# Block 2's attention in units of one query tile between projection steps, split value sums, and filter taps on ScalarE with adding DMAs

## The chip, the cores and the metric

The kernel runs on one core of a Trainium2 chip. The metric is the device time of one execution in microseconds (us). A core has five engines with a queue each: TensorE (PE) for matrix products, with its weight loads (PEld) shown apart; VectorE (DVE); ScalarE (ACT); GpSimd (POOL); and SyncE (SP), which here only starts transfers. Sixteen DMA engines move the data.

## What is computed

Two transformer blocks on 512 tokens of width 1024, in float32. Block 1 has an mLSTM and a sliding-window attention, a cross attention and a convolved feed-forward. Block 2 has four mixers of width 256 each that read the same projection, an output projection and a feed-forward. The change lies in block 2's mixers:

```
u_conf, u_sc, u_att, u_lru = split(rms_norm(x, pre_mix_g) @ w_in)
# conf: z = val * sigmoid(gate); causal depthwise filter of 31 taps; group norm; silu
y_a = conformer_conv_mixer(u_conf, ...)
# short conv: b_gate * causal_depthwise_conv(c_gate * xs, 3 taps)
y_b = short_conv_mixer(u_sc, ...)
# attention: 4 heads of width 64, blocks of 256 keys, slopes on the distance, causal
y_c = moba_attention(u_att)
# gated linear recurrence after a causal filter of 4 taps
y_d = rglru_mixer(u_lru, ...)
y = concatenate([y_a, y_b, y_c, y_d]) @ w_out
x = x + rms_norm(y, post_mix_g)
```

With 512 tokens there are two key blocks, and all earlier keys are attended to: the attention is a plain causal one of 512 by 512 with a bias by distance.

## The kernel before

**Split products.** A float32 product of full precision is made of three fp32r passes: each operand is split into a high part (`split`, line 112, on ACT) and the remainder (line 113, on DVE), and PE adds high x high, high x low and low x high (`mm3`, lines 138 to 140; `tm_phase`, lines 223 to 227). Weights come by SP's DMAs of 1 MB into three raw buffers and are split into five pairs of weight tiles (`split_w`).

**Block 2's mixers.** `X3` holds the normalised input, channels on partitions, split. `cm_phase` (from line 153) makes one column chunk of 128 outputs after the other: split its weights, 24 matmuls of 512 columns into one PSUM bank, then an evacuation function. The chunks are, in order: the filter's gates and values and the first recurrence gate (five, the first ones in halves), then the attention's queries and keys (`ATT`, four), the attention's values (`tm_block`), and nine in `rest`. The attention's score product is likewise split: the query tile `aq(h)` has the high half on 64 partitions and the low half on the other 64, and `ak(h)` gives two key tiles, so that two matmuls make a tile's scores. They live in the slots 0, 1, 4 and 5 of `H3`, the split concatenated mixer output, and in `akp`.

**The attention.** `at_head(h)` (line 1175) makes for four query tiles: two score matmuls, a reduction with bias and minimum on DVE (line 1185), the exponential with its sum on ACT (line 1187), reciprocal and normalisation on DVE (lines 1188 and 1189), transposes on PE with float32 operands (line 1192) and a copy out of PSUM, on DVE and ACT in turn (line 1193). Then four matmul groups in float32 (line 1243) add up a head's values; the trace shows each as two instructions. After each head some of the nine `rest` chunks are made (`cuts`), and the recurrence (`lru`), the group norm's mean (`conf_mean`) or its end (`conf_norm`).

**The filter.** `taps(c)` (line 1118) puts 31 DVE instructions for each of the two channel chunks into the list `bg`: each multiplies a shifted input `zp` by a weight and adds it to `acc`. `pump(n)` (line 149) writes the next n of them into the program; `cm_phase` calls it after each chunk, and the rest is written before `conf_mean`.

**What sets the order.** The program is written as a list of instructions for each engine and goes through a planner (`TileContext(schedule_with_timeline_sim=True)`, line 1401). It places the instructions by simulated time: the one written first goes first, but one written later may go ahead while the first is not ready in the plan. On the chip the order of an engine's queue is then fixed: an instruction that waits holds those behind it. Buffers of a tag (`bufs`) come round; whoever takes one waits until its last user is done.

**What follows.** `w_out` (line 1287, `tm_phase`) reads `H3` in the order of `order4`, slots 6, 7, 2, 3, 4, 5, 0, 1: recurrence, short convolution, attention, filter. Its first group is of two token tiles, with 12 matmuls for each slot. Of its eight weight tiles the last three are in the extra pool `wx4`.

Of the kernel before, what the change touches and what calls it, by code (L numbers as in the profile page):

```python
# [41 lines left out]
def tile_two_blocks(ctx: ExitStack, tc: tile.TileContext, a: dict, out: bass.AP, dbg=None):  # L42
# [988 lines left out]
    def tmp():  # L1031
        return mx.tile([P, T], F32, name="tmp", tag="tmp", bufs=6)
# [41 lines left out]
    cs, cx = {}, {}  # L1074

    def sc_c(c):
        def f(ps):
            cs[c], cx[c] = tmp(), tmp()
            act.activation(cs[c], ps, AF.Copy)
        return f  # L1080

    def sc_x(c):
        def f(ps):
            dve.tensor_mul(cx[c], cs[c], ps)
            w = pv[:, c, SCW:SCW + 3]
            act.activation(cs[c], cx[c], AF.Copy, scale=w[:, 2:3])
            for j in (1, 0):
                s = 2 - j
                dve.scalar_tensor_tensor(cs[c][:, s:], cx[c][:, :T - s], w[:, j:j + 1], cs[c][:, s:],
                                         op0=OP.mult, op1=OP.add)  # L1090
        return f

    def sc_b(c):
        def f(ps):
            dve.tensor_mul(cx[c], cs[c], ps)
            split(H3[0][:, 2 + c, :], H3[1][:, 2 + c, :], cx[c])
        return f
# [20 lines left out]
    def taps(c):  # L1118
        z, w = zp[c], half[:, c, :]
        bg.append(lambda: dve.tensor_scalar(acc[c], z[:, 0:T], w[:, 0:1], pv[:, c, DWB:DWB + 1],  # L1120
                                            op0=OP.mult, op1=OP.add))
        for j in range(1, 31):
            bg.append(lambda j=j: dve.scalar_tensor_tensor(acc[c], z[:, j:j + T], w[:, j:j + 1], acc[c],  # L1123
                                                           op0=OP.mult, op1=OP.add))
# [3 lines left out]
    def conf_mean():  # L1128
        for c in (1, 0):
# [22 lines left out]
    def lru(c):  # L1152
# [13 lines left out]
        dve.tensor_mul(lps[0], av_, av_)  # L1166
# [8 lines left out]
    def at_head(h):  # L1175
        pts = m2.tile([P, NT, T], F32, name="apts", tag="apts", bufs=1)
        for i in range(NT):
            n = (i + 1) * P
            s = psm.tile([P, T], F32, name="as", tag="s", bufs=2)
            m = max(n, 256)  # L1180
            for j in range(2):
                pe.matmul(s[:, :m], aq(h)[:, i * P:(i + 1) * P], ak(h)[j][:, :m], start=j == 0, stop=j == 1)
            L = m2.tile([P, T], F32, name="aL", tag="aL", bufs=2)
            st = m2.tile([P, 3], F32, name="ast", tag="ast", bufs=4)
            dve.tensor_tensor_reduce(L[:, :n], s[:, :n], ab[:, T - n:], scale=-0.25 ** (h + 1), scalar=-NEG,
                                     op0=OP.add, op1=OP.min, accum_out=st[:, 0:1])
            act.activation(L[:, :n], L[:, :n], AF.Exp, scale=-1.0, bias=st[:, 0:1], accum_out=st[:, 1:2])
            dve.reciprocal(st[:, 2:3], st[:, 1:2])
            dve.tensor_scalar(L[:, :n], L[:, :n], st[:, 2:3], None, op0=OP.mult)
            pt = psm.tile([P, NT, P], F32, name="apt", tag="pt", bufs=2)  # L1190
            for kb in range(i + 1):
                pe.transpose(pt[:, kb, :], L[:, kb * P:(kb + 1) * P], ident)
            (act.copy if i % 2 else dve.tensor_copy)(pts[:, 0:i + 1, i * P:(i + 1) * P], pt[:, 0:i + 1, :])
        return pts

# [3 lines left out]
    for c in (1, 0):  # L1199
        taps(c)  # L1200
# [13 lines left out]
    akp = m2.tile([P, 2, 2, T], F32R, name="akp")  # L1214
# [7 lines left out]
    av = m2.tile([P, NT, 256], F32, name="av")  # L1222
# [8 lines left out]
    rest = chunks[5:]  # L1231
    for c in range(2):
        rest += [(sc[c], sc_c(c)), (sx[c], sc_x(c)), (sb[c], sc_b(c))]
    cuts = (0, 3, 4, 6, len(rest))


    for c in range(2):
        o = psm.tile([P, T], F32, name="ao", tag="o", bufs=1)
        for e in range(2):
            h = 2 * c + e  # L1240
            pts = at_head(h)
            for kb in range(NT):
                pe.matmul(o[64 * e:64 * e + 64, kb * P:], av[:, kb, h * 64:(h + 1) * 64], pts[:, kb, kb * P:],
                          start=kb == 0, stop=kb == NT - 1)
            cm_phase(*MM, rest[cuts[h]:cuts[h + 1]], X3, 0, rate=RATE)
            if h in (0, 1):
                lru(h)
            if h == 2:
                pump(len(bg))
                conf_mean()  # L1250
            if h == 3:
                conf_norm()
        split(H3[0][:, 4 + c, :], H3[1][:, 4 + c, :], o)
# [151 lines left out]
```

## Time and profile before

| | us |
|---|---|
| median of 3 runs | 1320.43 |
| lowest and highest | 1320.33, 1323.15 |
| the profiled execution's own time | 1322.3 |
| its span, first to last instruction | 1320.6 |

The page of the profile gives busy times over the span, and the trace gives each instruction with its start, its length and, in brackets, the idle time of its engine just before it and what ended that. Matmuls follow one another faster than one lasts, so the cost of one is the distance between two starts. The granted clock is a share of TensorE's upper level: 1.00 is 2.4 GHz and 0.50 is 1.2 GHz. The mixers of block 2 stand at about 790 to 930 us.

### The profile page before, as it was taken

How to read it: one execution, taken by the hardware profiler on the slowest of the kernel's cores; microseconds unless marked ns; L12 is line 12 of the kernel's file. 1: busy time of each engine (PE TensorE's matmuls, PEld its weight loads, DVE VectorE, ACT ScalarE, POOL GpSimd, SP SyncE). 2: the span in 40 equal slices, each digit the busy share in tenths (PEclk: the TensorE clock that was granted, in tenths of full speed). 3: DMA queues.
4: the chain of work that ended last, by engine and by line, in shares of the span. 5: the costliest groups of instructions: out<-in, count | busy, mean ns of one | idle time of the engine just before them, and what ended most of it. 6: DMA issues, size and time to landing. Idle time of an engine off the chain costs nothing.

```text
span 1320.6 us, 17065 instructions
## 1 busy us (share of the span) xinstructions
PE 1300.4 (98%) x6918; PEld 1114.9 (84%) x6918; DVE 744.3 (56%) x1204; ACT 534.2 (40%) x895; POOL 76.1 (6%) x152
## 2 busy tenths in 40 slices
PE   8999999999999999999999999999999999999997
PEld 7899899899889888888888898767898888888886
DVE  5765877584666655556633569995453334532422
ACT  5664564333423433344422134576432223432311
POOL 3221020110000000000000120000100000000000
PEclk9999999998999999999999999999999999999999
DMA  8312344432223332313233124212234332223211
GB/s 255 108 65 73 104 144 160 181 109 97 97 96 116 124 128 64 128 64 128 70 122 128 32 69 138 73 45 93 73 93 125 96 96 97 96 96 112 96 46 51
DMA packets 92148, 134.87 MB, mean 102 GB/s; under 512 B 4572, under 2 KB 77329, under 8 KB 92062
## 3 DMA queue, kind: packets, MB, share of 16 engines
q1 hardware_dynamic: 90030, 129.09, 29.7%
q10 hardware_dynamic: 1384, 2.58, 0.6%
q0 software_dynamic: 656, 2.12, 0.5%
q8 instruction: 54, 0.88, 0.3%
q14 instruction: 24, 0.20, 0.0%
HBM read 131.66 MB, written 2.12 MB: 101 GB/s over the span
## 4 chain that ended last, share of the span: by engine, by line
PE 94%; DVE 3%; ACT 2%; issue 0%; DMA 0%; POOL 0%; SPq 0%; DVEq 0%; POOLq 0%; ACTq 0%
PE cm L139 15%; PE cm L138 15%; PE cm L140 15%; PE tm L224 9%; PE tm L223 9%; PE tm L227 9%; PE tmc L200 2%; PE tmc L201 2%; PE tmc L199 2%; PE tr L294 1%; PE tm L140 1%; PE tm L139 1%; PE tm L138 1%; PE num L680 1%; DVE cacc L1123 1%; PE mls L660 1%
## 5 line engine op out<-in xcount | busy, mean ns | idle before, releaser
L113 DVE TENSOR_TENSOR wl<-rawc,wh 128x1024 fp32r<-128x1024 f32 x140 | 170.7, 1222 | 203.6 <-ACT wh L112 203.3
L112 ACT ACTIVATE wh<-rawc 128x1024 fp32r<-128x1024 f32 x140 | 147.7, 1059 | 222.0 <-PE cm L139 190.8
L113 DVE TENSOR_TENSOR wl<-rawr,wh 128x1024 fp32r<-128x1024 f32 x73 | 88.9, 1223 | 147.4 <-ACT wh L112 147.4
L112 ACT ACTIVATE wh<-rawr 128x1024 fp32r<-128x1024 f32 x73 | 76.9, 1060 | 175.3 <-PE tm L227 126.6
L139 PE MATMUL cm<-x2l,wh 128*128 128x512 f32 (+1 forms) x392 | 143.8, 368 | 0.0
L140 PE MATMUL cm<-x2h,wl 128*128 128x512 f32 (+1 forms) x392 | 143.7, 367 | 0.0
L138 PE MATMUL cm<-x2h,wh 128*128 128x512 f32 (+1 forms) x392 | 143.1, 368 | 0.0
L139 PE MATMUL cm<-x4l,wh 128*128 128x512 f32 (+1 forms) x296 | 106.6, 361 | 1.3 <-DVE x4l L113 1.3
L140 PE MATMUL cm<-x4h,wl 128*128 128x512 f32 (+1 forms) x296 | 106.4, 360 | 0.0
L138 PE MATMUL cm<-x4h,wh 128*128 128x512 f32 (+1 forms) x296 | 105.9, 361 | 0.0
L140 PEld LDWEIGHTS cm<-x2h,wl 128*128 128x128 f32 x392 | 73.8, 189 | 12.1
L139 PEld LDWEIGHTS cm<-x2l,wh 128*128 128x128 f32 x392 | 73.8, 189 | 12.0
L138 PEld LDWEIGHTS cm<-x2h,wh 128*128 128x128 f32 x392 | 73.5, 189 | 12.3
L624 DVE SCALAR_TENSOR_TENSOR uy<-cm,fw,uy 128x511 f32<-128x511 f32 x88 | 65.5, 747 | 1.4
L138 PE MATMUL cm<-x3h,wh 128*128 128x512 f32 (+1 forms) x184 | 63.9, 352 | 1.1 <-DVE xc L624 0.8
L139 PEld LDWEIGHTS cm<-x4l,wh 128*128 128x128 f32 x296 | 55.8, 189 | 10.0 <-DVE x4l L113 1.5
L139 PE MATMUL cm<-x3l,wh 128*128 128x512 f32 (+1 forms) x184 | 64.1, 350 | 0.0
L140 PE MATMUL cm<-x3h,wl 128*128 128x512 f32 (+1 forms) x184 | 63.5, 347 | 0.0
L140 PEld LDWEIGHTS cm<-x4h,wl 128*128 128x128 f32 x296 | 55.8, 189 | 8.3
L138 PEld LDWEIGHTS cm<-x4h,wh 128*128 128x128 f32 x296 | 55.5, 189 | 8.5
L329 POOL TENSOR_TENSOR rs_r<-rs_e,mhalf 128x1 f32<-128x1 f32 (+1 forms) x16 | 24.2, 1510 | 540.5 <-DVE rs_e L328 540.5
L199 PE MATMUL tmc<-wh,xh 128*128 128x256 f32 (+1 forms) x160 | 47.2, 295 | 1.5 <-ACT wh L112 1.5
(457 smaller groups left out, 3058.2 us busy)
## 6 DMA issues: line engine op xcount, KB each, us to landing
rawc<-in_ffn_w_up_dram SPq DMA_DIRECT2D x22, 1024.0 KB
rawc<-in_w_in_dram SPq DMA_DIRECT2D x20, 1024.0 KB
rawc<-in_mlp_w_dram SPq DMA_DIRECT2D x16, 1024.0 KB
rawr<-in_mlp_w_dram SPq DMA_DIRECT2D x16, 1024.0 KB
rawr<-in_ffn_w_down_dram SPq DMA_DIRECT2D x11, 1024.0 KB
rawr<-in_w_out_dram SPq DMA_DIRECT2D x10, 1024.0 KB
rawc<-in_xa_wkv_dram SPq DMA_DIRECT2D x8, 1024.0 KB
rawc<-in_xa_wq_dram SPq DMA_DIRECT2D x4, 1024.0 KB
```

The costliest lines, as they stand in the source:

```text
L112: act.activation(hi, src, AF.Copy)
L113: dve.tensor_sub(lo, src, hi.bitcast(F32))
L138: pe.matmul(ps, wh, xh, start=first, stop=False)
L139: pe.matmul(ps, wh, xl, start=False, stop=False)
L140: pe.matmul(ps, wl, xh, start=False, stop=last)
L199: pe.matmul(o, xh, wh, start=k == 0, stop=False)
L200: pe.matmul(o, xh, wl, start=False, stop=False)
L201: pe.matmul(o, xl, wh, start=False, stop=k == KC - 1)
L223: pe.matmul(ps[t][h], xh, wh[:, c], start=i == 0, stop=False)
L224: pe.matmul(ps[t][h], xh, wl[:, c], start=False, stop=False)
L227: pe.matmul(ps[t][h], xl, wh[:, c], start=False, stop=i == n - 1)
L624: dve.scalar_tensor_tensor(dst[:, s:], ps[:, :T - s], w[:, j:j + 1], y[:, s:], op0=OP.mult, op1=OP.add)
```

## The change

The attention is made in 16 units of one head and one query tile. Turn u of a loop writes unit u's scores and softmax (`at_scores`), then 4 or 5 of the 72 projection steps of `rest` (`stream`, a step is three matmuls), the transposes of unit u-1 (`at_turn`), in each second turn the value sum of two tiles (`at_sum`), and two entries of `bg`. The normalisation goes from DVE to ACT. The transposed probabilities are split into two halves, and so are the values, which stand as 128 columns (64 high, 64 low): a matmul with them makes both halves' products at once, on the upper and the lower 64 partitions, and ACT and DVE add the two. Keys of heads 2 and 3 go to slots 2 and 3 of `H3` and `akp` falls away; the gates of the short convolution, whose result goes there, come last in `rest`.

Of the filter's 31 taps of channel chunk 1, sixteen are made by ACT into a buffer (two of them), and fifteen DMAs of GpSimd's queue add these to `accd`, into which the first tap goes directly; DVE adds `accd` to `acc[1]` ahead of the mean. In `bg` one such tap stands before each three of DVE's. `conf_mean` and `conf_norm` stand after all units. A square in `lru` goes from DVE to ACT, and `tmp` has five buffers for six.

```diff
+    accd = mx.tile([P, T], F32, name="caccd")
+    NDMA = {0: 0, 1: 16}
+
+    def dma_tap(z, w, j):
+        first = j == 31 - NDMA[1]
+        dst = accd if first else mx.tile([P, T], F32, name="ctap", tag="ctap", bufs=2)
+        act.activation(dst, z[:, j:j + T], AF.Copy, scale=w[:, j:j + 1])
+        if not first:
+            pool.dma_start(accd, dst, accum_op=OP.add)
...
+        while on_dve or on_dma:
+            bg.extend(on_dma[:1] + on_dve[:3])
+            del on_dma[:1], on_dve[:3]
...
     def conf_mean():
+        dve.tensor_add(acc[1], acc[1], accd)
...
-        dve.tensor_mul(lps[0], av_, av_)
+        act.activation(lps[0], av_, AF.Square)
...
     def ak(h):
-        return [H3[i][:, h, :] if h < 2 else akp[:, h - 2, i, :] for i in range(2)]
+        return [H3[i][:, h, :] for i in range(2)]
...
+    av = m2.tile([P, NT, 4, P], F32R, name="av")
+
     def av_evac(t0, ps):
-        act.activation(av[:, t0:t0 + 2, :], ps.rearrange("p (u c) -> p u c", u=2), AF.Copy)
+        v = av[:, t0:t0 + 2].rearrange("p u h d -> p (u h) d")
+        split(v[:, :, 0:64], v[:, :, 64:P], ps.rearrange("p (u d) -> p u d", d=64))
         pump(RATE)
...
+    rest = chunks[5:] + [(sc[0], sc_c(0)), (sx[0], sc_x(0)), (sc[1], sc_c(1)), (sx[1], sc_x(1)),
+                         (sb[0], sc_b(0)), (sb[1], sc_b(1))]
...
+    ptp = [m2.tile([P, 2, 2 * p + 2, 256], F32R, name=f"apts{p}") for p in range(2)]
+    for p in range(2):
+        pool.memset(ptp[p][:, :, 2 * p + 1, 0:P].bitcast(F32), 0.0)
...
+        act.activation(L[:, :n], L[:, :n], AF.Copy, scale=st[:, 2:3])
+        Ls[h, i] = L
+
+    def at_turn(h, i):
+        L = Ls.pop((h, i))
+        pt = psm.tile([P, NT, P], F32, name="apt", tag="pt", bufs=2)
+        for kb in range(i + 1):
+            pe.transpose(pt[:, kb, :], L[:, kb * P:(kb + 1) * P], ident)
+        d = ptp[i // 2][:, :, 0:i + 1, (i % 2) * P:(i % 2 + 1) * P]
+        split(d[:, 0], d[:, 1], pt[:, 0:i + 1, :])
+
+    def at_sum(h, p):
+        if p == 0:
+            os_[h] = psm.tile([P, T], F32, name="ao", tag="o", bufs=1)
+        o = os_[h]
+        for kb in range(2 * p + 2):
+            for i in range(2):
+                pe.matmul(o[:, p * 256:(p + 1) * 256], av[:, kb, h, :], ptp[p][:, i, kb, :],
+                          start=kb == 0 and i == 0, stop=kb == 2 * p + 1 and i == 1)
+        if p == 1:
+            c, e = h // 2, h % 2
+            if e == 0:
+                osum[c] = m2.tile([P, T], F32, name="aos", tag="aos", bufs=1)
+            r = osum[c][HALF[e], :]
+            act.copy(r, o[HALF[1 - e], :])
+            dve.tensor_add(r, o[HALF[e], :], r)
+            if e == 1:
+                split(H3[0][:, 4 + c, :], H3[1][:, 4 + c, :], osum[c])
+
+    units = [(h, i) for h in range(4) for i in range(NT)]
+    N = len(units)
+    done = 0
+    for u in range(N + 2):
+        if u < N:
+            at_scores(*units[u])
+        upto = min((u + 1) * len(rest) * KC // N, len(rest) * KC)
+        for _ in range(upto - done):
+            next(filler)
+        done = upto
+        if 1 <= u <= N:
+            at_turn(*units[u - 1])
+        if u >= 2 and u % 2 == 1:
+            at_sum(units[u - 2][0], units[u - 2][1] // 2)
+        pump(2)
+    for _ in filler:
+        pass
+    pump(len(bg))
+    conf_mean()
+    conf_norm()
```

## Rows read from the trace of the kernel before

**Rows 1.** The page: busy us, share of the span and instructions of each engine.
```profile
PE 1300.4 (98%) x6918; PEld 1114.9 (84%) x6918; DVE 744.3 (56%) x1204; ACT 534.2 (40%) x895; POOL 76.1 (6%) x152
```
**Rows 2.** Stretches: length, busy PE, PEld, DVE, ACT, POOL; granted clock, DMA share, GB/s.
```profile
798.00:826.00 28.00, 28.00 (x150) 24.23 (x149) 27.53 (x38) 13.73 (x20) 0.00 (x0) 1.00 0.41 134
826.00:911.84 85.84, 81.14 (x376) 61.63 (x374) 73.96 (x151) 50.84 (x87) 0.00 (x0) 0.98 0.19 66
...
862.00:864.00 2.00, 2.00 (x6) 1.59 (x5) 2.00 (x5) 0.00 (x0) 0.00 (x0) 0.50 0.00 0
```
**Rows 3.** PE in order of time: start, us, instructions [idle before <-releaser].
```profile
850.18 0.36 PE L1182 MATMUL as<-h3h,h3l 128*128 128x256 f32 x1
...
852.24 2.34 PE L1243 MATMUL ao<-apts,av 128*64 128x512 f32 x8 [1.34 <-DVE apts L1193]
...
860.09 0.70 PE L1192 MATMUL apt<-ident,aL 128*128 128x128 f32 x3 [2.28 <-DVE aL L1189]
861.61 0.63 PE L138 MATMUL cm<-x3h,wh 128*128 128x512 f32 x1 [0.82 <-DVE xc L624]
...
865.36 0.40 PE L138 MATMUL cm<-x3h,wh 128*128 128x512 f32 x1
```
**Rows 4.** The chain that ended last, in order of time: start, us, what.
```profile
872.14 0.23 PE cm L139
...
878.26 2.30 PE ao L1243 x8
```
**Rows 5.** PE in order of time: projections of 256 columns.
```profile
784.95 0.28 PE L138 MATMUL cm<-x3h,wh 128*128 128x256 f32 x1
785.07 0.28 PE L139 MATMUL cm<-x3l,wh 128*128 128x256 f32 x1
```
**Rows 6.** PE, then DVE, in order of time: scores and normalisation late in the stage.
```profile
901.18 0.89 PE L1182 MATMUL as<-akp,h3l 128*128 128x384 f32 x3
...
903.18 0.42 DVE L1189 TENSOR_SCALAR aL<-aL,ast 128x384 f32<-128x384 f32 x1
```
**Rows 7.** Groups of DVE, 826 to 912 us: busy us, mean ns of one, idle before.
```profile
L1123 DVE SCALAR_TENSOR_TENSOR cacc<-zp,half,cacc 128x512 f32<-128x512 f32 x35 | 25.1, 743 | 0.0
L1189 DVE TENSOR_SCALAR aL<-aL,ast 128x128 f32<-128x128 f32 (+3 forms) x16 | 5.9, 383 | 0.1
```
**Rows 8.** Groups of ACT, 826 to 912 us.
```profile
L1187 ACT ACTIVATE aL<-aL,ast 128x128 f32<-128x128 f32 (+3 forms) x16 | 8.9, 558 | 5.1 <-DVE ast L1185 5.1
L1193 ACT COPY apts<-apt 128x256 f32<-128x256 f32 (+1 forms) x7 | 3.2, 462 | 16.3 <-PE apt L1192 16.3
L1086 ACT ACTIVATE tmp<-tmp,pv 128x512 f32<-128x512 f32 x2 | 1.4, 711 | 0.0
```
**Rows 9.** GpSimd's DMAs (`mb`, then `swb`), then ACT's waits: total us, times, longest.
```profile
DMA to landing us min/median/max: 3.3/3.4/5.1
...
DMA to landing us min/median/max: 7.0/7.0/7.0
...
ACT mle L663 <- DMA mb<-mrow_d: 7.0, 3, 3.4
```
**Rows 10.** DVE, then POOL, in order of time: filter input and mask.
```profile
795.81 0.68 DVE L1046 SCALAR_TENSOR_TENSOR zp<-tmp,cm 128x512 f32<-128x512 f32 x1
...
780.09 0.66 POOL L1208 TENSOR_SCALAR_AFFINE_SELECT ab<-ab 128x128 f32<-128x128 f32 x1
```
**Rows 11.** The tail in order of time: chain, DVE, ACT, DVE, PE.
```profile
909.93 1.72 PE cva L1139 x4
...
920.22 1.47 DVE L113 TENSOR_TENSOR h3l<-cacc,h3h 128x512 fp32r<-128x512 f32 x2
...
921.73 2.96 ACT L112 ACTIVATE wxh<-rawr 128x1024 fp32r<-128x1024 f32 x3 [0.27 <-DVE h3l L113]
...
922.82 3.50 DVE L113 TENSOR_TENSOR wxl<-rawr,wxh 128x1024 fp32r<-128x1024 f32 x3 [0.53 <-ACT wxh L112]
...
928.99 0.39 PE L223 MATMUL tm<-wxh,h3h 128*128 128x512 f32 x1
```

More of the change, by code (lines that the diff above doesn't have):

```diff
@@ L1094, in f @@
         def f(ps):
-            dve.tensor_mul(cx[c], cs[c], ps)
-            split(H3[0][:, 2 + c, :], H3[1][:, 2 + c, :], cx[c])
+            dve.tensor_mul(cs[c], cs[c], ps)
+            split(H3[0][:, 2 + c, :], H3[1][:, 2 + c, :], cs[c])
         return f
@@ L1116, in tile_two_blocks, with taps @@
     acc = [mx.tile([P, T], F32, name=f"cacc{c}") for c in range(2)]
[L1118 to L1124, printed above, removed]
+    accd = mx.tile([P, T], F32, name="caccd")
[6 more added lines that the diff above has]
+            pool.dma_start(accd, dst, accum_op=OP.add)
+    def taps():
+        on_dve, on_dma = [], []
+        for c in (1, 0):
+            z, w = zp[c], half[:, c, :]
+            on_dve.append(lambda z=z, w=w, c=c: dve.tensor_scalar(acc[c], z[:, 0:T], w[:, 0:1], pv[:, c, DWB:DWB + 1],
+                                                                 op0=OP.mult, op1=OP.add))
+            for j in range(1, 31 - NDMA[c]):
+                on_dve.append(lambda z=z, w=w, c=c, j=j: dve.scalar_tensor_tensor(
+                    acc[c], z[:, j:j + T], w[:, j:j + 1], acc[c], op0=OP.mult, op1=OP.add))
+            on_dma += [lambda z=z, w=w, j=j: dma_tap(z, w, j) for j in range(31 - NDMA[c], 31)]
+        while on_dve or on_dma:
+            bg.extend(on_dma[:1] + on_dve[:3])
+            del on_dma[:1], on_dve[:3]
     sq, var = {}, {}
     def conf_mean():
+        dve.tensor_add(acc[1], acc[1], accd)
         for c in (1, 0):
@@ L1173, in lru @@
         split(H3[0][:, 6 + c, :], H3[1][:, 6 + c, :], xc[c])
[L1175 to L1194, printed above, removed]
     chunks = ([(cg[c], cgate_evac(c)) for c in range(2)] + [(cv[c], cval_evac(c)) for c in range(2)]
@@ L1198, in tile_two_blocks @@
     cm_phase(psl, "mm", 8, chunks[:5], X3, SK, fin)
-    for c in (1, 0):
-        taps(c)
+    taps()
     dump("x3", X)
@@ L1230, in tile_two_blocks @@
     tm_block(w_in2, 1792, X3, NT, *MM, av_evac)
[L1231 to L1253, printed above, removed]
+    rest = chunks[5:] + [(sc[0], sc_c(0)), (sx[0], sc_x(0)), (sc[1], sc_c(1)), (sx[1], sc_x(1)),
+                         (sb[0], sc_b(0)), (sb[1], sc_b(1))]
@@ new lines, in stream @@
+    def stream():
+        for n, (src, evac) in enumerate(rest):
+            w = split_w(src())
+            ps = psm.tile([P, T], F32, name="cm", tag="mm", bufs=3)
+            for k in range(KC):
+                mm3(ps, w[0][:, k, :], w[1][:, k, :], X3[0][:, k, :], X3[1][:, k, :], k == 0, k == KC - 1)
+                if k == KC - 1:
+                    evac(ps)
+                if (n, k) in ((2, KC - 1), (3, 3)):
+                    lru(n - 2)
+                yield
+    filler = stream()
@@ new lines, in tile_two_blocks, with at_scores @@
+    ptp = [m2.tile([P, 2, 2 * p + 2, 256], F32R, name=f"apts{p}") for p in range(2)]
+    for p in range(2):
+        pool.memset(ptp[p][:, :, 2 * p + 1, 0:P].bitcast(F32), 0.0)
+    Ls, os_, osum = {}, {}, {}
+    def at_scores(h, i):
+        n = (i + 1) * P
+        s = psm.tile([P, T], F32, name="as", tag="s", bufs=2)
+        m = max(n, 256)
+        for j in range(2):
+            pe.matmul(s[:, :m], aq(h)[:, i * P:(i + 1) * P], ak(h)[j][:, :m], start=j == 0, stop=j == 1)
+        L = m2.tile([P, T], F32, name="aL", tag="aL", bufs=2)
+        st = m2.tile([P, 3], F32, name="ast", tag="ast", bufs=4)
+        dve.tensor_tensor_reduce(L[:, :n], s[:, :n], ab[:, T - n:], scale=-0.25 ** (h + 1), scalar=-NEG,
+                                 op0=OP.add, op1=OP.min, accum_out=st[:, 0:1])
+        act.activation(L[:, :n], L[:, :n], AF.Exp, scale=-1.0, bias=st[:, 0:1], accum_out=st[:, 1:2])
+        dve.reciprocal(st[:, 2:3], st[:, 1:2])
+        act.activation(L[:, :n], L[:, :n], AF.Copy, scale=st[:, 2:3])
+        Ls[h, i] = L
```

15 lines of the change are left out of this document (7 added, 8 removed).

## The prediction

> **What bounds the kernel now.** I read the busy shares first. TensorE (PE) is busy for 98% of the span, with VectorE (DVE) at 56% and ScalarE (ACT) at 40% [rows 1]. So the time is PE's work plus the holes in it; another engine counts only where PE waits for it.
>
> Then I read the busy table by stretch for the stage that the change touches. From 798 to 826 us PE has no hole. From 826 to 911.84 us, where the four attention heads stand between the last nine column chunks, PE is busy 81.14 of 85.84 us, so 4.70 us are holes, and its mean granted clock is 0.98. DVE is busy 27.53 of 28.00 and 73.96 of 85.84 us there, ACT 13.73 and 50.84 [rows 2]. Over the whole execution DVE is half idle; in this stage it is the fullest engine beside PE.
>
> PE's timeline says where the holes lie. The values of head 0 start 1.34 us late behind DVE's copy of the transposed probabilities, a group of transposes 2.28 us late behind DVE's normalisation, a projection 0.82 us late behind DVE's convolution [rows 3]. All three releasers are DVE: its queue is full of filter taps and the small attention steps come out late. Behind these holes the granted clock falls to half, the 1.2 GHz level (0.50 from 862 to 864 us) [rows 2], and nine matmuls from 861.61 to 865.36 us take 3.75 us where a spacing of 0.23 us at full clock [rows 4] would make 2.1 [rows 3]. That is another 1.7 us, so stalls of 6.4 us in all.
>
> **The change part by part.**
>
> *Values.* The probabilities and values become fp32r halves. A head's sum before is eight instructions in 2.30 us [rows 4], so 9.2 us for four heads. After it is twelve matmuls of 256 columns a head. The projections' 256-column matmuls, each with its own weight load, follow at 0.12 us [rows 5], so 4 x 12 x 0.12 = 5.8 us. PE loses 3.4 us. The 32 score matmuls, 40 transposes, the recurrence's and the group norm's matmuls and the projections stay as they are.
>
> *Pipeline.* Sixteen units (head, query tile) now go round with 4.5 projection steps (24 x 0.23 / 8 = 0.69 us each, so 3.1 us) between them; a unit's transposes come one unit later and its sum another one. From a unit's scores to its transposes PE has two such fillers, some 7 us with the small work. The way through reduction, exponential, reciprocal and normalisation took 2.4 us where DVE had room (scores from 901.18, the last normalised by 903.60), and 9.9 us where its queue was full (850.18 to the transposes at 860.09) [rows 3, 6]. So the holes can close: gain from 0 to 6.4 us, before what is late next.
>
> *DVE.* It loses 16 taps at 0.743 us (11.9), 16 normalisations (5.9) [rows 7] and two squares (1.4 at a tap's length or a little less). It gains the lower halves of eight more transposed tiles (3.7 at the 0.462 of ACT's copy), the values' (1.4), four half sums and one sum of the two filter parts (3.5). 101.5 us become about 91, in a stage that shrinks from 113.8 to 104.8 (4.7 + 1.7 + three of the four value blocks at 0.87; the fourth lies behind 912).
>
> *ACT.* It gains 16 normalisations, nearest the exponential's 0.558 us (8.9); eight more copies at 0.462 (3.7); four half copies (1.8); two squares at 0.711 (1.4); 16 taps at 0.711 (11.4) [rows 8]: 27.2 us. Its 64.6 us become about 92 of 104.8, and if half of the taps run before 826 us, 72.3 of 76.8 us after it, 94%. The table loads I leave as they are: from the exponential to gelu, to the square root and back are the same switches. ACT takes DVE's place as the fullest engine. I price what that makes late between 0 and the 6.4 us that DVE, at 86% over the same stretch, makes now, and take 3.5, just over the middle, since the pipeline's 7 us cover most of the way but ACT is fuller than DVE was.
>
> *Adding DMAs.* Fifteen DMAs of 256 KB from GpSimd's queue add into one tile, so each waits for the one before it. The trace has no adding DMA. Its nearest row is the 256 KB broadcast of block 1, 3.4 us from issue to landing; the longest on that queue is 7.0 us for 1 MB [rows 9]. The chain is 51 to 105 us and starts when the input of the filters' second half is there, at 796.5 us [rows 10]; it ends between 848 and 902 us, before the group norm needs its sum at about 903. I take the short end, and no cost on the path. "DMA: Bandwidth & Descriptors" in the Trainium skill (Anatomy of one DMA) gives 2.0 us and the bytes at 436 GB/s, by which 256 KB would be 2.6 us, an estimate, and the chain 39 us; the row is slower than that. Queued behind a DMA's wait on GpSimd there is only the zeroing of the two probability tiles; the trace runs such setup early, the mask's selection at 780.09 us [rows 10], so no cost; if it stood behind DMAs, the first sum would wait for some of them, 3.4 us each.
>
> *The wait that is added.* A tap on ACT needs one of two buffers, so from the fourth tap on ACT waits until an earlier DMA has landed, and the weight splits, exponentials and evacuations queue behind it. That is the second rival.
>
> *Tail.* The group norm now comes after all units. Its chain from the variance at 909.93 us to the last lower half at 921.69 is 11.8 us, and the extra weight tiles are split right behind it, from 921.73, for a matmul at 928.99 [rows 11]; the first is whole at about 924.0, so there are 5 us in hand. After, the mean, square and variance (about 4 us) no longer lie ahead of w_out, so the hand is empty: cost 0 to 3 us, and I take 0, since the adding chain ends early and the taps may. The last short-convolution gate waits for head 3's scores, as its place holds that head's keys; w_out reaches it 5 us later and needs 2 us of it. Fewer temporaries and the other order of the chunks I cost at nothing under the same filler.
>
> *Sum.* -3.4 (values) - 6.4 (stalls) + 3.5 (what ACT makes late) = -6.3 us. The profiled execution took 1322.3 us, its span 1320.6 and 1.7 around it; less 6.3 that is 1316.0. It stands 1.9 us above the median of the runs shown, 1320.4, so I predict 1314.
>
> **The rivals.**
>
> 1. *The stalls only change their engine.* ACT at 94% is as late as DVE was, 6.4 us, and the tail's chain costs 2 more: 1320.4 - 9.8 + 8.4 = 1319. For it speaks that three engines then stand near 90% in one stage; against it the filler between all units, which before came in blocks after whole heads. It wins if PE's holes stay above 7 us.
>
> 2. *ACT stands still for the DMAs (slower).* ACT's order is fixed, and its taps stand where the planner thinks that a buffer is free. In block 1 ACT waited 7.0 us in three times for the 256 KB broadcasts, 2.3 us each [rows 9], so a planned place can be too early. Thirteen taps waiting 2.3 us hold ACT for 30 us; ACT has about 13 free (104.8 - 92), so 17 us reach PE: 1320.4 - 9.8 + 17 = 1328. It costs something from 1 us a wait on, and the change is slower than before from 1.8 us a wait. For it: those waits, and a price that no row shows. Against it: ACT was at leisure there, and the units ask for a tap only in every second one, some 9 us apart (76.8 us for 16 units). "SBUF — State Buffer" in the Trainium skill (Who interferes with whom) says that DVE in a two-port mode keeps GpSimd from writing descriptors, and names copy and tensor_scalar. Sixteen normalisations of that form leave DVE here, so by that rule the second rival gets no help; no run yet shows it.
>
> 3. *The adding chain ends late.* If an adding DMA takes over 7.1 us, the sum comes after 903, and w_out waits in its first group; at 8 us each by some 13 us: 1327. It is weaker, as 7.0 us is the row of four times the bytes.
>
> 4. *The pass saves nothing on PE.* If the split matmuls ran at the old rate the 3.4 us would be missing: 1317.5. The 0.12 us rows speak against it.
>
> **How the numbers follow.** Forecast 1314: 0.50, its own range 1310.5 (no new lateness) to 1318. Stalls change engine, 1319: 0.20. ACT held, 1328: 0.20. Late chain, 1327: 0.05. No saving on PE: 0.05. About 0.2%, 2.6 us, is what a measurement of this kernel can tell from no change: faster ends at 1317.8, slower begins at 1323.1. Faster takes the forecast, the fourth and a part of the first, less the forecast's upper edge: 0.53. Slower takes the second and third, less their light ends: 0.23. The rest is 0.24. The range goes from 1310 to 1328; it leaves out waits of over 2.3 us and a better end than the sum without lateness.
>
> **What would show it.** In the trace after: 48 value matmuls of 256 columns at 0.12 us; no hole of PE behind DVE's normalisation, as there is none; the clock at its upper level over the stage; holes under 4 us in sum, their releasers on ACT. Adding DMAs landing in 3 to 7 us, the last before 900. Wrong would be the forecast if ACT shows idle time ended by an adding DMA of more than 1 us a tap, if w_out's first group waits for the group norm or the extra weight tiles, or if PE's holes are larger than the 4.7 us of now.

## The result and the profile after

The changed kernel takes 1344.84 us (median of 4 runs, 1342.38 to 1345.2) where the kernel before took 1321.79 beside it: 1.0168 times as long over all runs, 95% interval 1.0153 to 1.0183. By the medians it is 23 us slower; the prediction was 1314, in a range of 1310 to 1328. Single runs of one kernel lie up to some 6 us apart, and a part of that is seen outside the change: between 318 and 330 us, in block 1, the granted clock falls to 0.50 in some profiled executions (3.4 us lost in before and after, 5.1 in e1 below) and stays at 1.00 in others (e17), so whole times are compared as ratios over all runs, and the sums below are of the stage alone.

The busy times of the page after, which answer to [rows 1]:

```profile
PE 1306.3 (97%) x6934; PEld 1122.2 (84%) x6934; DVE 737.8 (55%) x1185; ACT 561.0 (42%) x943; POOL 88.6 (7%) x169
```

They tell little of 23 us. The table by stretch does; here it is for the kernel after, with the columns of [rows 2]: length, busy PE, PEld, DVE, ACT, POOL, then granted clock, DMA share, GB/s.

```profile
798.00:826.00 28.00, 26.06 (x118) 21.48 (x117) 20.87 (x28) 11.88 (x18) 4.41 (x5) 0.94 0.63 154
826.00:840.00 14.00, 11.56 (x92) 11.12 (x91) 10.21 (x18) 9.32 (x15) 2.58 (x3) 1.00 0.63 145
...
854.00:868.00 14.00, 9.41 (x36) 6.94 (x36) 10.02 (x21) 10.27 (x19) 2.58 (x3) 0.76 0.67 171
868.00:882.00 14.00, 6.47 (x22) 3.78 (x23) 9.44 (x21) 8.06 (x17) 0.00 (x0) 0.76 0.19 52
...
966.00:980.00 14.00, 10.22 (x50) 8.35 (x49) 12.12 (x17) 8.97 (x20) 3.07 (x4) 0.97 0.49 150
980.00:1000.00 20.00, 19.69 (x144) 19.16 (x143) 11.11 (x16) 7.15 (x18) 1.63 (x3) 0.85 0.00 1
```

No engine is full in these stretches: from 826 to 882 us VectorE (DVE) stands at 9 to 10 of 14 us where it stood at 12 to 14 before, ScalarE (ACT) at 8 to 10, and TensorE (PE) has holes all the same. From 798 to 1008 us PE's holes are 22.4 us (6.0 before), and the lower clock takes up to 11.9 us (1.7 before; in each stretch its length times the missing share of the clock). That is 16.4 us more of holes and up to 10.2 more of slow clock; less the 3.4 us of the value sums it makes 23.2, about the difference. The clock's part is an upper bound, as it counts time in which PE stood still too: of the 11.9 us, 8.9 fall on time in which PE was busy (by windows of 0.5 us; 1.7 of 1.7 before). Nearly all lies in two places: 798 to 882 us, and behind 966 us, where w_out is over.

Why engines with room leave PE waiting is in the waits of ACT (total us, times, longest) and in its timeline:

```profile
ACT ctap L1126 <- DMA caccd<-ctap: 21.0, 10, 7.9
```
```profile
806.30 0.73 ACT L1126 ACTIVATE ctap<-zp,half 128x512 f32<-128x512 f32 x1 [0.30 <-DMA caccd<-ctap]
814.95 0.72 ACT L1126 ACTIVATE ctap<-zp,half 128x512 f32<-128x512 f32 x1 [7.93 <-DMA caccd<-ctap]
815.70 0.68 ACT L1059 ACTIVATE h3l<-cm,qscale 64x512 fp32r<-64x512 f32 x1
```

ACT stands 21.0 us before taps whose buffer an adding DMA still reads. A busy share doesn't count that time. The longest wait can be followed through the engines. The query evacuation (815.70) is queued behind the tap; DVE's half of it starts 6.18 us late, and PE 1.94 us late behind DVE. DVE, then PE, in order of time:

```profile
816.42 0.76 DVE L1060 SCALAR_TENSOR_TENSOR h3l<-cm,qscale,h3l 64x512 fp32r<-64x512 f32 x1 [6.18 <-ACT h3l L1059]
```
```profile
817.32 0.47 PE L138 MATMUL cm<-x3h,wh 128*128 128x512 f32 x1 [1.94 <-DVE h3l L1060]
```

GpSimd's timeline shows why a buffer is held so long: its DMAs go one at a time.

```profile
806.78 0.87 POOL L1128 DMA_DIRECT2D caccd<-ctap  x1 [6.86 <-DMA caccd<-ctap]
815.39 0.85 POOL L1128 DMA_DIRECT2D caccd<-ctap  x1 [7.74 <-issue]
...
844.74 0.86 POOL L1128 DMA_DIRECT2D caccd<-ctap  x1 [2.98 <-DMA caccd<-ctap]
848.55 0.86 POOL L1128 DMA_DIRECT2D caccd<-ctap  x1 [2.96 <-DMA caccd<-ctap]
...
865.84 0.86 POOL L1128 DMA_DIRECT2D caccd<-ctap  x1 [3.35 <-DMA caccd<-ctap]
```

A step of the chain is 3.8 us in most places: 0.86 us to issue and 2.98 us until the landing lets the next one go. The first two lie beside 1 MB weight loads (from 800 to 814 us) and take twice that, 7.8 and 8.6 us. From issue to landing the view of this tile gives, against [rows 9]:

```profile
DMA to landing us min/median/max: 3.3/3.3/8.1
```

The chain's end makes the largest hole, and here it is not ACT that is held but DVE. DVE's addition of the finished sum stands in the middle of its queue; it waits 3.46 us for the last DMA, the reciprocal of a softmax is queued behind it, and PE's transposes come 5.06 us late. DVE, then PE:

```profile
871.54 0.69 DVE L1147 TENSOR_TENSOR cacc<-cacc,caccd 128x512 f32<-128x512 f32 x1 [3.46 <-DMA caccd<-ctap]
872.14 0.16 DVE L1264 RECIPROCAL ast<-ast 128x1 f32<-128x1 f32 x1
```
```profile
872.79 0.47 PE L1272 MATMUL apt<-ident,aL 128*128 128x128 f32 x1 [5.06 <-ACT aL L1265]
```

The granted clock is 0.50 from 870 to 876 us, in this hole and behind it.

The value sums do what was forecast. Eight matmuls stand from 905.80 to the next projection at 906.74, 0.118 us each; the forecast from [rows 5] was 0.12:

```profile
905.80 1.11 PE L1282 MATMUL ao<-apts,av 128*128 128x256 f32 x8
906.74 0.40 PE L138 MATMUL cm<-x3h,wh 128*128 128x512 f32 x1
```

### The profile page after: what moved, and what is told of

The parts are those of the page before. It is cut to its first block, busy times and chain, and to the rows that moved or that the text cites. A ratio compares the mean times of both kernels' runs of the same rounds, so it can differ in the third digit from the quotient of the medians.

```text
span 1343.3 us, 17163 instructions
## 1 busy us (share of the span) xinstructions
PE 1306.3 (97%) x6934; PEld 1122.2 (84%) x6934; DVE 737.8 (55%) x1185; ACT 561.0 (42%) x943; POOL 88.6 (7%) x169
## 5 line engine op out<-in xcount | busy, mean ns | idle before, releaser
L139 PEld LDWEIGHTS cm<-x2l,wh 128*128 128x128 f32 x392 | 73.8, 189 | 11.9
```

Source lines behind the costliest of these rows:

```text
L139: pe.matmul(ps, wh, xl, start=False, stop=False)
```

## The experiments

My theory after the result was that ACT, held by the buffers, is the whole loss (A). The rivals were that the pipeline is slow by itself, in the middle of the stage (C) or behind it (B, later D), and that the sixteen taps overfill ACT. Ratios are to the kernel before on the same chip. Holes and slow clock are in us from 798 to 1008 us of one profiled execution each, worked out as above.

| kernel | ratio to before (95%) | holes | slow clock up to |
|---|---|---|---|
| before | 1 | 6.0 | 1.7 |
| after | 1.0168 (1.0153 to 1.0183) | 22.4 | 11.9 |
| e1: no adding DMAs | 1.0044 (1.0028 to 1.0060) | 11.5 | 6.7 |
| e3: old attention, adding DMAs | 1.0120 (1.0102 to 1.0137) | 17.6 | 8.4 |
| e7: seven taps, two buffers | 1.0098 (1.0077 to 1.0119) | 16.6 | 8.4 |
| e7: seven taps, six buffers | 1.0048 (1.0033 to 1.0063) | 10.7 | 6.9 |
| e8: e1, early mean | 1.0039 (1.0019 to 1.0060) | 11.7 | 6.9 |
| e9: six buffers, early mean | 1.0033 (1.0021 to 1.0045) | 11.8 | 6.9 |
| e10: GpSimd adds | 1.0101 (1.0086 to 1.0116) | 17.8 | 12.0 |
| e11: after, early mean | 1.0171 (1.0156 to 1.0186) | 22.1 | 17.1 |
| e12: e1, mean and end of the group norm early | 1.0023 (1.0010 to 1.0037) | 10.6 | 6.7 |
| e13: e12, units ahead | 1.0027 (1.0016 to 1.0037) | 9.0 | 5.2 |
| e14: e8, half the taps left out | 0.9994 (0.9984 to 1.0004) | 7.2 | 5.0 |
| e15: e1, early mean, more filler early | 1.0078 (1.0060 to 1.0097) | 14.6 | 10.2 |
| e16: e1, heads in blocks | 0.9995 (0.9979 to 1.0010) | 6.9 | 5.0 |
| e17: e1, early mean, late units ahead | 0.9993 (0.9982 to 1.0004) | 8.1 | 3.4 |
| e18: e16, seven taps, six buffers | 1.0007 (0.9998 to 1.0016) | 9.3 | 3.4 |
| e19: e17, recurrences later | 1.0020 (1.0010 to 1.0030) | 9.4 | 1.7 |

### What the adding DMAs cost: e1, e3, e7

e1 puts all 62 taps back on DVE; e3 is the kernel before with only the taps of the change. The two runs with seven taps differ in the buffers alone.

```diff
# e1 (and no accd)
-    NDMA = {0: 0, 1: 16}
+    NDMA = {0: 0, 1: 0}
# e7, two buffers
+    NDMA = {0: 0, 1: 7}
# e7, six buffers: as that, and each added tap has its own
...
+        elif n == 1: dst = m2.tile([P, T], F32, name="aL", tag="aL", bufs=2)
+        elif n == 6: dst = m2.tile([P, T], F32, name="aos", tag="aos", bufs=1)
+        elif n in (4, 5): dst = xc[n - 4]
...
```

> All 31 taps of both filter chunks on DVE as before, no ACT taps, no adding DMAs; the rest of the change stays. Theory A (ACT stands still until adding DMAs free its buffers): the 21 us of such waits are gone and with them PE's holes and slow clock; DVE is about as full as before, so 1314 to 1322 us, PE holes under 6 us. Theory B (the pipeline of units itself loads ACT too much): still 1335 us or more, with PE waiting for ACT's softmax steps as in the changed kernel.

> The kernel before with nothing changed but the filter: sixteen ACT taps, fifteen adding DMAs, two buffers. Theory A: ACT is held as in the changed kernel: 1333 to 1345 us. Theory B (attention part is to blame): DVE is relieved and ACT has room, 1312 to 1320 us.

> Seven taps of chunk 1 instead of sixteen go to ACT, six adding DMAs, two buffers as in the changed kernel. Theory A: ACT still waits for the first DMAs, which are the slow ones (7.9 us in one wait), some 10 to 12 us of the 21; about 1328 to 1334 us. Theory B: 1335 to 1345 us, since only nine taps (6.4 us) leave ACT.

> As the one with seven ACT taps, but each of the six added taps has a buffer of its own (places that are free at that time), so ACT never waits for a DMA. Same ACT work, same DMAs. Theory A: no ACT idle time ended by an adding DMA, 10 us or more faster than its twin with two buffers: 1314 to 1322 us. Theory B: the same time as its twin within 3 us.

Without the DMAs the change is at 1.0044, with them at 1.0168: 1.2%, some 16 us. On the old attention the same taps cost 1.2% too, so the two parts of the change add up. ACT's waits in e3, then in e7 with two buffers:

```profile
ACT ctap L1124 <- DMA caccd<-ctap: 20.5, 10, 7.8
```
```profile
ACT ctap L1126 <- DMA caccd<-ctap: 11.3, 4, 8.2
```

With six buffers ACT has no such wait, and six DMAs still run one behind the other: 1.0048, no different from none at all (1.0044). It is 5.9 us faster than its twin with two buffers; A had asked for 10 or more, B for 3 at most. So six DMAs and seven taps on ACT cost nothing that can be measured, net of the 5.2 us that leave DVE, and the wait for a buffer does: 0.5% for 11.3 us of it.

With sixteen taps a second cost is added, the hole at the chain's end. In both kernels with seven taps DVE doesn't wait for the last DMA; in after it waits 3.46 us (above), and in e3 5.09 us, with 7.26 us of PE behind it. DVE, then PE, of e3:

```profile
864.98 0.69 DVE L1145 TENSOR_TENSOR cacc<-cacc,caccd 128x512 f32<-128x512 f32 x1 [5.09 <-DMA caccd<-ctap]
```
```profile
868.41 3.75 PE L1173 MATMUL lps<-xc,bd 128*128 128x512 f32 x4 [7.26 <-issue]
```

The same stretch of e1, beside the one of after at the top (6.47 us busy, clock 0.76):

```profile
868.00:882.00 14.00, 14.00 (x64) 11.05 (x63) 12.74 (x24) 10.18 (x21) 0.00 (x0) 1.00 0.20 75
```

So after has 7.5 us of holes and up to 3.4 us of slow clock here that e1 has not, and at 798 to 868 us only 3.8 and up to 1.7 us more than e1. A holds for the kernels with seven taps and for a part of the 16 us; the chain's end makes another part, by the traces not the smaller one. How the 16 us divide isn't shown by a run, as none has sixteen taps with enough buffers or the sum read later. That the taps' work overfills ACT is excluded for seven taps only; for sixteen, ACT's 70% in after (826 to 911.84 us) speaks against it. As the whole story A falls in any case: e1 should have been faster than before, and is 6 us slower.

### GpSimd adds in place of the DMAs: e10

The mean stands early here, which changes little by itself (e11, below).

```diff
-            pool.dma_start(accd, dst, accum_op=OP.add)
+            pool.tensor_add(accd, accd, dst)
```

> The changed kernel with all 16 taps on ScalarE and two buffers, but GpSimd adds each of the 15 to the sum by an instruction of its own (128x512 float32) in place of an adding DMA, and conf_mean stands after unit 11. If ScalarE was held because an adding DMA keeps a buffer for 3.8 us and more, an addition that takes 0.6 to 2 us (no row shows it; 128x512 iota on this engine 0.56) sets ScalarE free: 1317 to 1323, no wait of ScalarE for a buffer of over 1 us. If the sixteen taps' own work (11.4 us) on a full ScalarE is the loss, it stays near 1330 to 1338, and ScalarE shows no wait for buffers.

1.0101, and ACT waits only 4.3 us for buffers, 1.5 at the longest. DVE's groups of 794 to 826 us, then GpSimd's of 794 to 828:

```profile
L1137 DVE SCALAR_TENSOR_TENSOR cacc<-zp,half,cacc 128x512 f32<-128x512 f32 x17 | 20.6, 1256 | 0.1
```
```profile
L1128 POOL TENSOR_TENSOR caccd<-caccd,ctap 128x512 f32<-128x512 f32 x15 | 24.5, 1631 | 24.2 <-ACT ctap L1126 23.2 <-POOL caccd L1128 0.3
```

A tap on DVE takes 1256 ns beside GpSimd's additions and 743 ns otherwise [rows 7]. Neither branch expected this. The time, 1336.1 us, lies in the range of the second, but PE's three longest waits here (3.8, 3.8 and 2.4 us) name DVE's part of the evacuations, and not ACT: the additions are short enough for the buffers, and DVE pays. "SBUF — State Buffer" in the Trainium skill (Who interferes with whom) states that a VectorE instruction with two SBUF inputs and a GpSimd instruction that reads SBUF block one another; these rows agree.

### Where the pipeline itself loses: e8, e9, e11, e12

In e1 two places differ from before: the holes at 840 to 868 us, where DVE is full, are larger (6.1 us, 4.7 before), and there is a hole behind w_out. PE's waits (798 to 1000 us) and two stretches of e1:

```profile
PE tr L294 <- DVE hx L991: 4.0, 1, 4.0
PE as L1256 <- DVE ast L1259: 2.6, 1, 2.6
```
```profile
854.00:868.00 14.00, 9.07 (x33) 6.46 (x34) 14.00 (x32) 12.43 (x25) 0.00 (x0) 0.76 0.01 1
...
952.00:966.00 14.00, 9.46 (x47) 7.49 (x45) 12.94 (x17) 8.08 (x16) 1.70 (x3) 0.92 0.49 150
```

I took the second for the late group norm (B) and wrote its mean earlier in three kernels (and in e10); e12 also has the norm's end ahead of the last units.

```diff
         pump(2)
+        if u == 11:        # e8, e9, e10, e11; e12: 9
+            pump(len(bg))
+            conf_mean()
+        if u == 12:        # e12 only
+            conf_norm()
...
-    pump(len(bg))
-    conf_mean()
-    conf_norm()            # e12 only
```

> The changed kernel without the adding DMAs (no tap on ScalarE, all 62 on VectorE), as before at 1326.9, and in addition the rest of the taps and conf_mean stand after unit 11 instead of after all units; conf_norm stays at the end. Theory B: most of the 6 us by which the pipeline alone was slower than the kernel before lies behind the stage: the group norm's chain, written after all units, finishes late (last lower half at about 928 us where it was 921.7), TensorE then goes on with other groups of w_out, and at its end transposes wait 4.0 us for the last rows, with a slow clock behind it (0.92 and 0.84 in 952 to 980). By it: 1321 (1319 to 1322.5), and no wait of a transpose for hx of over 2 us. Theory C: the loss is in the pipeline's own holes at 840 to 868 us, where VectorE stays full (6 us of holes and a clock of 0.76); the early mean adds to VectorE's load there, so 1326 to 1329.

> Seven taps on ScalarE, six adding DMAs, each added tap with a buffer of its own, as before at 1327.5, and in addition the rest of the taps and conf_mean after unit 11. Theory B (late group norm): 1321 to 1323. Theory C (holes of the pipeline with full engines): 1326 to 1328, since these taps took little from the holes before.

> The changed kernel whole (16 taps on ScalarE, 15 adding DMAs, two buffers), only with conf_mean and the rest of the taps after unit 11. If the late group norm and the held ScalarE cost one beside the other: 1344.8 - 6 = about 1338 to 1340. If the held ScalarE delays the adding chain (its end at 871 us) so that the early mean is itself late, VectorE's queue stands behind the last sum: 1343 or more.

> The changed kernel without adding DMAs (all 62 taps on VectorE), with the group norm's mean after unit 9 and its end after unit 12, so that its logarithms, exponentials and their table loads on ScalarE (1.28 us each) stand ahead of the last units instead of between the last unit's exponential and its normalisation. Theory D: the loss behind the stage is a chain of the last unit. In the variant with the early mean alone (1327.3) the last unit's exponential ran at 913.07 and its normalisation at 919.16, with two table loads between; the last half sum came at 927.9, and only then were the extra weight tiles of w_out split (929.2, before 921.7), as they take the memory that the attention's tiles leave; TensorE filled in with w_out's later groups and stood 4.2 us for the last rows at the end. By D the splits begin at 923 to 926 and part of the 6.5 us behind 952 us comes back: 1322 to 1325. Rival C (holes at 840 to 868, VectorE full) alone: no change, 1326 to 1328.

B falls: e8, e9 and e11 are within the noise what they were without the early mean, and the wait for hx is there (4.2, 4.7 and 4.7 us). ACT's timeline of e8 led to the next theory (D). Between the last unit's exponential and its normalisation stand two table loads for the group norm's logarithm and exponential, and the extra weight tiles of w_out are split only at 929.17 (921.73 before, [rows 11]):

```profile
913.07 0.72 ACT L1261 ACTIVATE aL<-aL,ast 128x512 f32<-128x512 f32 x1
...
914.95 1.28 ACT L1158 ACT_TABLE_LOAD   x1
...
917.33 1.28 ACT L1160 ACT_TABLE_LOAD   x1
...
919.16 0.71 ACT L1263 ACTIVATE aL<-aL,ast 128x512 f32<-128x512 f32 x1
...
929.17 2.94 ACT L112 ACTIVATE wxh<-rawr 128x1024 fp32r<-128x1024 f32 x3
```

With the norm ahead of the last units (e12) the splits begin at 927.7 and the wait for hx stays at 3.8 us; the time is 0.2% better than e1's, which the intervals don't tell apart. The table loads are not the cause of that wait.

### The order behind the stage: e13, e15, e17

These change how many projection steps stand between the units. None has adding DMAs; the mean stands after unit 9 in e13 and e15 and after unit 10 in e17.

```diff
-        upto = min((u + 1) * len(rest) * KC // N, len(rest) * KC)
+        upto = min((u + 1) * 60 // N, len(rest) * KC)                                            # e13, else as e12
+        upto = min((u + 1) * 11 // 2 if u < 8 else 44 + (u - 7) * 2, len(rest) * KC)              # e15
+        upto = min((u + 1) * 9 // 2 if u < 8 else 36 + (u - 7) * 3, len(rest) * KC)               # e17
```

> As the run with the early group norm (mean after unit 9, end after unit 12, no adding DMAs), and the units take 3.75 projection steps each in place of 4.5, so that some 8 us of projections are left when the last unit's scores are made. By D the extra weight tiles are split by 922 us and no transpose waits over 2 us for hx: 1319 to 1322. Against it: the units then come faster (2.6 us of projections each) in the stretch where VectorE is full with taps, so the holes at 840 to 868 us grow (rival C): 1325 or more, with more than 8 us of holes there.

> The changed kernel without adding DMAs, mean after unit 9, end of the group norm after all; the first eight units take 5.5 projection steps each, the last eight two each, and some eight to twelve steps are left behind the last unit. If both holes of the pipeline have the causes found so far (too little filler where VectorE is full with taps; the last unit too late for w_out's order), the holes at 840 to 868 shrink from about 6 to 3 us, no transpose waits over 2 us for hx, and it is 1317 to 1321. If fewer steps between the late units open holes there (run e13 showed 2.7 us at 882 to 896 with 3.75 steps), 1322 to 1326.

> The changed kernel without adding DMAs, mean after unit 10, end of the group norm after all; the first eight units with 4.5 projection steps as in the change, the last eight with three, so that twelve steps are left behind the last unit. Theory D': w_out's first group of two token tiles has seven slots without the last attention slot, 7 x 12 x 0.227 = 19 us; where that slot is later than this behind w_out's first matmul, TensorE takes other groups first, all rows end together, and a transpose waits about 4 us for hx with a slow clock behind it. Here the distance should be 8 to 17 us: no wait for hx over 1 us, clock 1.00 in 952 to 980, and with the holes at 840 to 868 unchanged (about 6 us) 1320 to 1323. If the wait for hx has another cause, it stays at 1326 to 1328.

In e13 the wait for hx is gone, and holes open in the middle (8.46 of 14 us busy at 854 to 868, 11.33 at 882 to 896), as its second branch said. e15, at 1332.9 us, is slower than both its branches: the distance below is 19.4 us and the wait for hx 4.7 us, and the middle holes grew too. Laid side by side, the kernels order by one number: the time from w_out's first matmul to the last half of the attention's output, the slot that w_out reads sixth. Before it was 9.8 us. In after, e1, both e7, e8 to e12, e14 and e15 it is 18.3 to 25.8 us, and each has a wait of 3.8 to 4.7 us for hx; in e3 (10.3), e13 (4.3), e16 (17.2) and e18 (13.5) there is none, and in e19 (17.4) two short ones of 1.1 us together. The change-over lies near the 19 us of work that w_out's first group has without that slot (7 slots x 12 x 0.227, an estimate). My reading is that with a later slot PE goes on with other groups, the first rows end late, and too little is left to cover the norm of the second token tile: in e1 the first rows' norm starts at 943.98 us, in before at 937.07, though e1 begins w_out 3.8 us earlier. e17 tested it. PE and DVE of e1, then of e17:

```profile
908.03 0.80 PE L223 MATMUL tm<-wh,h3h 128*128 128x512 f32 x1
...
930.03 0.69 DVE L113 TENSOR_TENSOR h3l<-aos,h3h 128x512 fp32r<-128x512 f32 x1 [0.70 <-ACT h3h L112]
```
```profile
907.56 0.80 PE L223 MATMUL tm<-wh,h3h 128*128 128x512 f32 x1
...
919.61 0.69 DVE L113 TENSOR_TENSOR h3l<-aos,h3h 128x512 fp32r<-128x512 f32 x1 [0.70 <-ACT h3h L112]
```

22.0 us become 12.1, the wait for hx is gone, the clock from 952 to 980 us is 1.00, the first rows' norm starts at 933.23 us, and the ratio falls from 1.0044 to 0.9993: 0.5%, 6.7 us. The early mean, which e17 has too, did nothing alone (e8).

### The middle, and the pipeline undone: e14, e16, e18, e19

e14 leaves out 30 taps of DVE. e16 has no adding DMAs, keeps the split values and the normalisation on ACT and puts the four tiles of a head together again, with the mean behind head 2's chunks; e18 adds the seven taps with six buffers to it. e19 is e17 with the two recurrences written later and seven temporaries in place of five.

```diff
# e14
-            for j in range(1, 31 - NDMA[c]):
+            for j in range(1, 16):
# e16 (the loop over units goes)
+    cuts = (0, 3, 4, 7, len(rest))
+    for h in range(4):
+        for i in range(NT):
+            at_scores(h, i)
+            at_turn(h, i)
+            if i % 2 == 1:
+                at_sum(h, i // 2)
...
+        if h == 2:
+            pump(len(bg))
+            conf_mean()
# e19
-                if (n, k) in ((2, KC - 1), (3, 3)):
-                    lru(n - 2)
+                if (n, k) in ((4, 3), (6, 3)):
+                    lru(0 if n == 4 else 1)
```

> The variant with the early mean and no adding DMAs (1327.3), and taps 16 to 30 of both filter channel chunks are left out (30 instructions of 0.743 us on VectorE, 22 us; this part of the filter is missing in the result). By rival C the holes at 840 to 868 us (6 us and about 3.4 us of slow clock) come from VectorE's full queue and go: 1317 to 1320, TensorE busy for the whole of 840 to 868. By theory D alone the loss behind 952 us stays as it is, the wait of a transpose for hx of about 4 us among it. If the holes stay with VectorE at leisure, the pipeline's own chain (scores, VectorE, ScalarE twice, transposes) is too long for its filler, and it stays at 1324 or more.

> The changed kernel without adding DMAs and without the pipeline: the four tiles of a head stand together again, each tile's transposes right behind its softmax, and whole column chunks between the heads (three, one, three, two), five taps after each chunk, the mean after head 2's chunks. The split values, the split probabilities, the half sums and the normalisation on ScalarE stay. If the pipeline's order is what cost (holes at 840 to 868 us, then w_out's groups out of order), this is the kernel before less the 3.4 us of the values, with holes of some 5 us as before: 1318 to 1321. If the split halves' added work on VectorE and ScalarE (8 more half copies, the values' halves, the half sums) is what cost, it stays at 1325 to 1329, as with the pipeline (1326.9).

> The heads in blocks (as in the run that undoes the pipeline, ratio 0.9995), and seven taps on ScalarE with six adding DMAs, each added tap with a buffer of its own: VectorE has 5.2 us less. If VectorE's full queue makes the holes of that kernel (some 6 us at 840 to 874), part goes: 1317 to 1321, and this would be the one that beats both. If the adding DMAs cost something even with buffers for all (the weights' transfers beside them), or the holes come from the recurrences' chains whatever the taps are, it is 1322 to 1326.

> As the last run of the pipeline (no adding DMAs, late units with three steps, ratio 0.9993), and the two recurrences stand after projection steps 35 and 51 in place of 23 and 27, so some 880 us and later, where VectorE's taps are done; seven temporaries in place of five. If the recurrences' chains among the units are what makes the holes at 840 to 868 us (6 us, and a clock of 0.76 in 14 us, 3.4 us), TensorE is busy there for over 26 of 28 us and it is 1314 to 1319, faster than both kernels. If the taps alone fill VectorE there, the holes shrink little, and the recurrences' halves come later, close to w_out's first matmul, which reads them first: 1321 to 1326.

e16 is the clearest: with the pipeline undone and no adding DMAs, the rest of the change costs nothing that can be measured, 0.9995 (1323.5 us, between its branches, beside 1322.5 for before). But its holes (6.9 us) and slow clock (5.0) are no smaller than with the pipeline put right (e17: 8.1 and 3.4), and no smaller than before. So the filler between the units closes nothing here, and in e16 the 3.4 us of the values are eaten by 0.9 us more of holes and up to 3.3 us more of slow clock than before.

What makes the middle holes is told apart in part. Without 30 taps (22 us of DVE) they shrink and the kernel gains 0.45% on e8; at 1321.6 us it lies between its branches, for with DVE busy only 9.41 of 14 us at 854 to 868 a hole of 2.64 us stays, before scores that wait for DVE's reduction. A full DVE is thus not the whole of it. Moving the recurrences empties the place and fills another. Two stretches of e19:

```profile
854.00:868.00 14.00, 13.50 (x67) 10.47 (x66) 13.26 (x27) 8.04 (x17) 0.00 (x0) 1.00 0.23 75
...
896.00:910.00 14.00, 10.85 (x49) 8.16 (x48) 8.68 (x18) 12.01 (x23) 0.00 (x0) 0.88 0.16 42
```

At 854 to 868 us PE is busy for 13.50 us (10.52 in e17) with DVE nearly as full as before, and between 868 and 910 us there are 7.0 us of holes (none in e17). In this run the holes go with the recurrences. Relief of 5 us on DVE by seven taps on ACT (e18) doesn't help. No kernel beats the one before by more than can be measured.

## Why the prediction was wrong

Three terms failed. The adding DMAs, taken at no cost, cost 16 us, by a held ACT and by a sum read too early. The tail, taken at 0, cost 6.7 us. The stalls that were to shrink by 2.9 us net grew by 3.7. The saving on PE's own work was right.

*Values, -3.4 us.* Right, by the spacing above.

*Pipeline, stalls of 6.4 us that close.* This step failed. The filler of 7 us was compared with the way through the softmax, and taken as cover. e17, the pipeline without its two faults, still has 6.1 us of holes and up to 3.4 us of slow clock ahead of 952 us. The releasers of [rows 3] had been read rightly as DVE's full queue, but the units go through the same queue: the chain got longer where the filler did.

*ACT, +3.5 us for what it makes late.* The net of both terms, -2.9, should be seen in e1, and there it is 6.7 + 3.4 less 4.7 + 1.7 us, +3.7. ACT's work was not the main cause, though: in e1 DVE is at 14.00 of 14 us in 854 to 868 us, and PE's waits of the middle name DVE for 3.9 us and ACT for 2.8. The work itself was sized well, as ACT's busy time grew by 26.8 us (27.2 forecast), but not its share of the stage: after has ACT busy for 60.25 of 85.84 us at 826 to 911.84, 70% and not 94%, and 9.8 us of its idle time there are waits for a buffer.

*The wait that is added.* This step failed: the wait was named and described rightly, and left out of the sum. The rival priced it at 13 waits of 2.3 us and 17 us on PE; the trace has 10 waits of 21.0 us in all, and the runs give the adding DMAs 16 us, of which this wait is a part. That the rival's 17 us come so near is partly luck, as it did not count the chain's end. Two reasons were given against it, and both fail: that ACT's waits in block 1 fell into its leisure and so say little (2.1 us a wait here, 2.3 there), and that a tap comes only every 9 us. The planner put the first taps side by side at 797 to 815 us, among the evacuations, and just beside the 1 MB weight loads, where an adding DMA took up to 8.1 us. The forecast took this wait at zero while its own chain of DMAs (at least 51 us for 15) said that a buffer is free only every 3.4 us.

*Adding DMAs.* The chain took 72 us, from 798.95 to about 871, well inside the 51 to 105; the short end was taken, and no cost on the path. This failed too. The chain ended in time for 903, but the sum was read at 871: DVE's addition stood there in its queue, with a softmax behind it, which cost 5.06 us of PE and a clock of 0.50 until 876 us. The third rival looked for a late chain in w_out only. No run changes that hole alone. The row of 3.4 us was a good price for one DMA (3.3 at the median), though not for a step of the chain (3.8). "DMA: Bandwidth & Descriptors" in the Trainium skill (Anatomy of one DMA) gave 2.6, an estimate; the measurement is 3.3, and decides. That GpSimd's zeroing runs early was right.

*Tail, 0 to 3 us, taken at 0.* This step failed, and by a mechanism that was not in it: 6.7 us, and not the group norm (e8, e12), but the attention's last slot, which I had not priced at all. I asked when the slots' producers end, and not what PE does while it waits.

*The sum.* -3.4 - 2.9 became -3.4 (values) + 3.7 (middle) + 6.7 (behind w_out) + 16 (adding DMAs: held ACT and the chain's end) = +23.0, with terms from e1, e17 and the ratios. The last two are known to some 3 us either way (from the intervals of the ratios), so it is in part chance that the sum meets the 23 us so closely.

## What to carry to other kernels

Before a slow consumer is fed from a fast engine's queue, compare how often a buffer comes free with how often the producer asks: every wait for a buffer stops all that is queued behind it, and the engine's busy share hides it; give it as many buffers as the chain has steps (shown here for six), or leave it. And ask where the consumer of the chain's result stands in its own queue: if it comes out before the chain is done, it stops that queue as well. When work is spread out evenly, look at what the next stage reads last and how long the stage can run without it. In these runs a hole behind a full queue moved with the work that fills the queue; spreading other work around it didn't close it.

## What the runs showed of the hardware

In after an adding DMA of 256 KB within SBUF lands in 3.3 us at the median, no longer than the broadcast of [rows 9], a chain of them makes most steps in 3.8 us, and beside 1 MB weight loads one takes up to 8.1 us. DVE's taps slow down from 743 to 1256 ns beside GpSimd's tensor additions of 1631 ns, but not beside its DMAs (742 ns in after, 826 to 912 us). In after the clock fell to 1.2 GHz (0.50 from 870 to 876 us) in and behind a hole of PE that began at 867.7 us, and to a mean of 0.85 from 980 to 1000 us, behind the holes of 966 to 980 us: all in all up to 10 us more than before, on top of 16 us more of holes.
